# Two token parts of 256 and 288 columns instead of 272 and 272 in a hybrid decoder layer

## The chip, the cores and the metric

The kernel runs on one NeuronCore of a Trainium2 chip. The metric is the device time of one execution in microseconds; the median of three runs before the change is 886.1 us (883.63 to 886.37). TensorE (PE) multiplies matrices, VectorE (DVE) and ScalarE (ACT) do elementwise work and copy results out of PSUM, GpSimd (POOL) does small copies, and SyncE (SP) issues the DMAs.

## The reference

One layer with two gated branches runs side by side on 512 prompt tokens and on 8 x 4 sample tokens (each of 8 requests brings four). Together that is 544 tokens of 1,024 features in float32.

```
shift, scale, gate = split(silu(c) @ w_cond + b_cond, 3)
h = x * (1 + scale) + shift
qa, ka, va, za, qkv_b, zb, a_b, b_b, ga, gb = split(h @ w_in)     # 1024 x 11280
o_a = dilated window attention, 3 groups of 8 heads, mixed by their softmax denominators
o_b = gated delta rule on silu(conv4(qkv_b)), 8 heads of 128, in chunks of 64
ya, yb = o_a * silu(za), rmsnorm(o_b) * silu(zb)
merged = sigmoid(ga) * (ya @ w_branch_a) + sigmoid(gb) * (yb @ w_branch_b)
x = layernorm(ALPHA * x + gate * (merged @ w_out))
```

The new caches and states of both branches are outputs too.

## The kernel before

**Data.** Tokens lie along the free dimension. h is held as two float32r tiles, `hhi` and `hlo` (128 partitions, 8 blocks of features, 544 tokens): the rounded value and the rest. Each weight tile of 128 x 1,024 is split in the same way into `hi` (ScalarE) and `lo` (VectorE). A product in full precision is then three matmuls per block of features: hhi with hi, hlo with hi, hhi with lo.

**Products.** `stream` (line 1043) works through a list of jobs, one for each tile of 128 output columns of `w_in` (85 on h) and one for each tile of the two branch products (8 on `yb`, 8 on `ya`). A job cuts its 544 tokens into two parts of 272 columns, because a `pp` tile has 512 columns. For each part it takes a PSUM bank from `pp` (two banks, lines 36 and 811), runs 8 x 3 matmuls into it (4 x 3 for `ya`), and calls the job's `evac`, which copies or combines the part while the other part runs. The same two parts are used for the first head's three column tiles and the small a/b product at the start (lines 961 to 997).

**What follows a part.** For the convolution (`conv_job`, line 1221 on), part 0 goes to `ext` as 272 columns; part 1 goes as 240 prompt columns and 32 sample columns, which land in another place. For attention (`attention_job`, line 1543 on), queries, keys and values of the prompt go into tiles of 512 tokens, for the two dilated groups in another order of tokens (17 and 15 blocks of 16), and the 32 sample tokens go to `qs`, `ks`, `vs`. Gates and branch products (`za_job`, `zb_job`, `gate_job`, `branch_job`) use `half(t, n)`, the same cut of a 544-wide tile.

**Order.** Every instruction is recorded first. A planner (`schedule`) then simulates all engines with its own cost of each instruction (for a float32r matmul of n columns `0.455e-3 * n + 0.002` us, line 390) and writes out one order per engine. Attention, the delta rule and the gates are generators with ranks; their pieces go between the matmuls of the jobs when their inputs are due. The output product at the end works on 128 tokens at a time, 512 or 256 columns wide, and does not use the two parts.

All instructions are issued by the line 727, which writes the recorded order, so the profile names that line throughout and tiles have to be told apart by name.

Of the kernel before, what the change touches and what calls it, by code (L numbers as in the profile page):

```python
# [13 lines left out]
AF = mybir.ActivationFunctionType  # L14
# [9 lines left out]
NTD = 4  # L24
NS = NB * NTD
NT = SEQ + NS
HF = NT // 2
PROJ = 11280
OFF_Q, OFF_K, OFF_V, OFF_ZA, OFF_B, OFF_ZB, OFF_AB, OFF_GA, OFF_GB = (
    0, 1536, 3072, 4608, 5120, 8192, 9216, 9232, 10256)  # L30
# [749 lines left out]
def body(ctx, tc, io):  # L780
    rec = Recorder()
    pe, ve, se, ge, sp = rec.engines()
# [28 lines left out]
    def pp():  # L811
        return psp.tile([128, 512], F32, name="pp", tag="pp")
# [30 lines left out]
    qs = keep.tile([128, 4, 3, NS], F32, name="qs")  # L843
    ks = keep.tile([128, 4, 3, NS], F32, name="ks")
    vs = keep.tile([128, 4, 3, NS], F32, name="vs")
# [41 lines left out]
    n = CONST[2].shape[1]  # L887
# [4 lines left out]
    abT = op.tile([128, NT], F32, name="abT", tag="o")[0:32]  # L892
    xs = xT[:, :, SEQ:].rearrange("p k (b t) -> p k b t", t=4)
    per_token = lambda t, k, n: t[:, k:k + n, 1:9, None].to_broadcast([128, n, 8, 4])
    cols_of = lambda n: slice(n * HF, (n + 1) * HF)
    with ExitStack() as fctx:
        fr = pool(fctx, "front", 1)
        cT = fr.tile([128, KT, 9], F32, name="cT")
# [59 lines left out]
            return pv[:, :, 0:9], bT[:, 8 * part + at:8 * part + at + m, None].to_broadcast([128, m, 9])  # L958

        x1 = [fr.tile([128, KT, NT], F32R, name=f"x1{u}") for u in "hl"]  # L960
        sums = [[f()[:, :HF] for _ in range(2)] for f in (pp, pd, pg)]
        for b, (c, m) in enumerate(CHUNKS):
            pv, bias = cond_block(1, c, m, b % 2)
            kk = slice(c, c + m)
# [9 lines left out]
            hi, lo = (wsp.tile([128, D], F32R, name=n, tag=n)[:, 0:384 * m].rearrange("p (k c) -> p k c", k=m) for n in ("hi", "lo"))  # L974
            se.activation(hi, W3[:, kk, 0:384], AF.Copy)
            ve.tensor_sub(lo, W3[:, kk, 0:384], hi.bitcast(F32))
            for k in range(c, c + m):
                for t in range(3):
                    w, w_ = (x[:, k - c, 128 * t:128 * t + 128] for x in (hi, lo))
# [7 lines left out]
        hl = fr.tile([128, KT, 32], F32R, name="hl")  # L987
        se.activation(hl[:, :, 0:16], W3[:, :, 384:400], AF.Copy)
        ve.tensor_sub(hl[:, :, 16:32], W3[:, :, 384:400], hl[:, :, 0:16].bitcast(F32))
        ps = [pg(), pg()]  # L990
        for n in range(2):
            for k in range(KT):
                for x in range(2):
                    pe.matmul(ps[n][0:32, :HF], hl[:, k], x1[x][:, k, cols_of(n)],
                              start=(k == 0 and x == 0), stop=(k == KT - 1 and x == 1))
        for n in range(2):
            se.activation(abT[:, cols_of(n)], ps[n][0:32, :HF], AF.Copy)
        for c, m in two_by_two:
            pv, bias = cond_block(0, c, m, c % 4)
            kk = slice(c, c + m)  # L1000
# [2 lines left out]
        ps, pv = pg(), pb_()  # L1003
# [39 lines left out]
    def stream(until):  # L1043

        while done[0] < until:
            i = done[0]
            job = jobs[i]
            for x in range(i, min(i + 5, len(jobs))):
                if x not in raws:
                    raws[x] = wraw.tile([128, D], F32, name="wt", tag="wraw")  # L1050
                    jobs[x].load(raws[x])
                if x <= i + 1 and x not in weights:
                    weights[x] = split(raws[x], jobs[x].nk * 128, ve)
            if job.start:
                yield job.start
            if job.begin:
                job.begin()
            (hi, lo), (xhi, xlo) = weights.pop(i), job.x
            for n in range(2):
                ps = pp()[:, :HF]  # L1060
                cols = slice(n * HF, (n + 1) * HF)
                for k in range(job.nk):
                    a, b = hi[:, k * 128:(k + 1) * 128], lo[:, k * 128:(k + 1) * 128]
                    for w, x in ((a, xhi), (a, xlo), (b, xhi)):
                        pe.matmul(ps, w, x(k)[:, cols], start=(k == 0 and w is a and x is xhi),
                                  stop=(k == job.nk - 1 and w is b))
                    if k < job.nk - 1:
                        yield 0
                job.evac(n, ps)
                if n and job.after:  # L1070
                    job.after()
                if not n:
                    yield 0
            done[0] += 1
            threads.set(job.over, 0.0)
            yield 0
# [4 lines left out]
    def column_job(name, **kw):  # L1081
        return Job(name[0], lambda raw: sp.dma_start(raw, io["w_in"][TILE_AT[name]]), KT, of_h, **kw)

    half = lambda t, n: t[:, n * HF:(n + 1) * HF]


    moves = [(g, b, r, min(r + MOVE, w - 4)) for g, (w, _) in enumerate(GROUPS) for b in range(8) for r in range(0, w - 4, MOVE)]
# [133 lines left out]
    def conv_job(h, s):  # L1221


        hd, tl, t = heads[h], s * 8 + h, {}

        def begin():
            if s == 1:
                hd.cx = dl.tile([128, 81], F32, name="cx")
                hd.stc = dl.tile([128, 3, 8, 3], F32, name="stc")
                sp.dma_start(hd.stc, io["state_conv"][:, h])  # L1230
                hd.KQ = dl.tile([128, 4, 2, 128], F32, name="KQ", bufs=3)
            if s == 2:
                hd.uv = dl.tile([128, 4, 128], F32, name="uv", bufs=1)

        def head_of_ext():
            t["ext"] = ext = dl.tile([128, 571], F32, name="ext")
            ge.memset(ext[:, 0:3], 0.0)
            es = ext[:, 515:571].rearrange("p (b w) -> p b w", w=7)
            ge.tensor_copy(es[:, :, 0:3], hd.stc[:, s])

        def evac(n, ps):
            if not n:
                head_of_ext()
                se.activation(t["ext"][:, 3:275], ps, AF.Copy)
                return
            ext = t["ext"]
            es = ext[:, 515:571].rearrange("p (b w) -> p b w", w=7)
            se.activation(ext[:, 275:515], ps[:, 0:240], AF.Copy)
            se.activation(es[:, :, 3:7], ps[:, 240:272].rearrange("p (b t) -> p b t", t=4), AF.Copy)
            convolve()  # L1250

        def shifted(raw, by):
            head_of_ext()
            ext = t["ext"]
            es = ext[:, 515:571].rearrange("p (b w) -> p b w", w=7)
            ve.tensor_scalar(ext[:, 3:515], raw[:, :SEQ], by[:, 0:1], None, op0=OP.add)
            ve.tensor_add(es[:, :, 3:7], raw[:, SEQ:].rearrange("p (b t) -> p b t", t=4),
                          by[:, 1:9, None].to_broadcast([128, 8, 4]))
            convolve()

        def convolve():
            ext, acc, cx = t["ext"], dl.tile([128, 572], F32, name="acc"), hd.cx
            u = hd.uv if s == 2 else hd.KQ[:, :, 1 - s, :]
            es = ext[:, 515:571].rearrange("p (b w) -> p b w", w=7)
            ge.tensor_copy(cx[:, s:9:3], ext[:, 512:515])
            ge.tensor_copy(cx[:, 9:81].rearrange("p (b t u) -> p u b t", t=3, u=3)[:, s], es[:, :, 4:7])
            se.activation(acc[:, 0:568], ext[:, 0:568], AF.Copy, scale=cw[:, tl, 0:1])
            for i in range(1, 4):
                ve.scalar_tensor_tensor(acc[:, 0:568], ext[:, i:i + 568], cw[:, tl, i:i + 1], acc[:, 0:568],
                                        op0=OP.mult, op1=OP.add)  # L1270
            se.activation(ext[:, 0:568], acc[:, 0:568], AF.Tanh, scale=0.5)
            ve.scalar_tensor_tensor(u, cols128(ext[:, 0:512]), 1.0, cols128(acc[:, 0:512]), op0=OP.add, op1=OP.mult)
            ve.scalar_tensor_tensor(us[:, s, h].rearrange("p (b t) -> p b t", t=4),
                                    win7(ext, 515), 1.0, win7(acc, 515), op0=OP.add, op1=OP.mult)
            if s != 1:
                threads.set(hd.v if s == 2 else hd.kq, 12.0)

        start = ()
        if s == 1 and h > 2:
            start = (heads[h - 3].freed,)  # L1280
        if s == 2 and h:
            start = (heads[h - 1].blocks,)
        job = column_job(("b", h, s), evac=evac, begin=begin, start=start)
        job.shifted = shifted
        return job
# [257 lines left out]
    def attention_job(j, g, s):  # L1543

        def begin():
            pairs[j][s, g] = spare()[:, :SEQ] if s == 2 else ap.tile([128, 512], F32, name="qk"[s], bufs=3)

        def evac(n, ps):
            t, scale = pairs[j][s, g], 1.0 if s else -0.125
            if g == 0:  # L1550
                lo, hi = ((0, 272), (272, 512))[n]
                se.activation(t[:, lo:hi], ps[:, 0:hi - lo], AF.Copy, scale=scale)
            else:
                v = t.rearrange("p (r a n) -> p n a r", r=4, a=4)
                m = (17, 15)[n]
                se.activation(v[:, 17 * n:17 * n + m], ps[:, 0:16 * m].rearrange("p (n a r) -> p n a r", a=4, r=4),
                              AF.Copy, scale=scale)
            if n:
                se.activation((qs, ks, vs)[s][:, j, g if s else at_g(g), :], ps[:, 240:272], AF.Copy, scale=scale)
                if s == 2:  # L1560
                    threads.set(ready[j, g], 2.5)

        return column_job(("a", j, g, s), evac=evac, begin=begin, start=(freed[j - 1] if j else began,))
# [954 lines left out]
```

## Time and profile before

| | |
|---|---|
| three runs | 883.63, 886.1, 886.37 us |
| span of the profiled execution | 886.1 us |
| mean granted TensorE clock | 0.995 |
| DMA, mean rate over the span | 267 GB/s |
| ScalarE activation table loads | 32, 41.1 us |

A group of a profile's page reads: line, engine, operation, output and inputs by the program's names, shape, count, then busy time in us, the mean duration of one in ns, and the engine's idle time just before them with what ended it. "L727 PE MATMUL pp<-hhi,lo" is a matmul into a `pp` bank with `hhi` streaming and `lo` as weights; 128x272 is partitions by columns of the stream. A matmul's duration reaches from its start to its modelled end and overlaps with the next one's. A row of the timeline begins with the start in us from the begin of the span and the duration in us.

### The profile page before, as it was taken

To read this page: it belongs to the slowest core of one execution; us is meant where nothing else is said; L and a number is where in the kernel's file an instruction comes from. 1 tells how busy PE (TensorE), PEld (TensorE's weight loads), DVE (VectorE), ACT (ScalarE), POOL (GpSimd) and SP (SyncE) were. 2 spreads that over 40 slices of the span, in tenths; PEclk is the share of its full clock that TensorE was granted. 3 is DMA by queue.
4 is the path that set the end of the run, shared out by engine and by line. 5 is a ranking of instruction groups with operands and counts; after the bars stand their busy time and mean duration, and the time that the engine had idled before them with its cause. 6 is when DMAs were issued, how large, how long until landed. Compare 5 with 4: busy or idle time off the path is not lost.

```text
span 886.1 us, 20733 instructions
## 1 busy us (share of the span) xinstructions
PE 864.7 (98%) x8176; PEld 818.1 (92%) x8176; DVE 643.4 (73%) x1330; ACT 451.7 (51%) x1073; POOL 68.7 (8%) x167
## 2 busy tenths in 40 slices
PE   8999999999999999999999999999999999999994
PEld 7889999898999899999999988999899999999884
DVE  4675557564458899968999753556899699998547
ACT  3546656765546696347775446732442222324324
POOL 0120110110001110002120000021010000001000
PEclk9999999999999999999999999999999999999998
DMA  9876768666687886889877885479869899987973
GB/s 334 337 212 199 234 219 268 235 206 214 198 256 249 282 278 207 271 265 329 303 227 257 262 291 186 169 219 293 330 223 375 275 402 420 377 285 235 348 248 142
DMA packets 121069, 236.18 MB, mean 267 GB/s; under 512 B 49174, under 2 KB 76640, under 8 KB 118284
## 3 DMA queue, kind: packets, MB, share of 16 engines
q1 hardware_dynamic: 120972, 234.86, 79.0%
q8 instruction: 64, 1.05, 0.5%
q14 instruction: 33, 0.27, 0.1%
HBM read 218.53 MB, written 103.97 MB: 364 GB/s over the span
## 4 chain that ended last, share of the span: by engine, by line
PE 82%; DMA 6%; DVE 5%; ACT 5%; issue 1%; SPq 1%; POOL 0%; DVEq 0%; ACTq 0%
PE pp L727 62%; PE pg L727 9%; PE pd L727 7%; PE pb L727 4%; DMA wc<-in_w_cb 2%; ACT L727 1%; DVE r L727 1%; DMA slab<-in_ks 1%; DMA dO<-orow 1%; DMA S<-in_state_delta 1%; DMA wv<-dw 1%; ACT hi L727 1%; DMA out_kv_s<-in_cache 1%; SPq L727 1%; ACT sq L727 1%
## 5 line engine op out<-in xcount | busy, mean ns | idle before, releaser
L727 PE MATMUL pp<-hhi,hi 128*128 128x272 f32 x1360 | 400.2, 294 | 1.7 <-DVE zt L727 1.0
L727 PE MATMUL pp<-hhi,lo 128*128 128x272 f32 x1360 | 401.3, 295 | 0.0
L727 PE MATMUL pp<-hlo,hi 128*128 128x272 f32 x1360 | 398.1, 293 | 0.0
L727 PEld LDWEIGHTS pp<-hhi,hi 128*128 128x128 f32 x1360 | 257.0, 189 | 4.6 <-issue 1.8
L727 PEld LDWEIGHTS pp<-hhi,lo 128*128 128x128 f32 x1360 | 256.7, 189 | 2.1 <-issue 1.4
L727 PEld LDWEIGHTS pp<-hlo,hi 128*128 128x128 f32 x1360 | 257.1, 189 | 1.5 <-issue 0.4
L727 ACT ACTIVATE hi<-wt 128x1024 fp32r<-128x1024 f32 (+1 forms) x101 | 103.6, 1026 | 171.2 <-PE pp L727 130.1
L727 DVE TENSOR_TENSOR lo<-wt,hi 128x1024 fp32r<-128x1024 f32 (+1 forms) x101 | 119.0, 1178 | 74.9 <-ACT hi L727 74.4
L727 DVE SCALAR_TENSOR_TENSOR acc<-ext,cw,acc 128x568 f32<-128x568 f32 x72 | 58.0, 805 | 1.6 <-ACT acc L727 0.6
L727 DVE TENSOR_TENSOR slab<-slab 128x512 f32<-128x512 f32 (+1 forms) x66 | 43.1, 669 | 6.7 <-DMA slab<-in_ks 4.5
L727 DVE TENSOR_REDUCE slab<-slab 128x8 f32<-128x512 f32 (+2 forms) x66 | 42.7, 660 | 3.3 <-ACT slab L727 3.0
L727 ACT ACT_TABLE_LOAD x32 | 41.1, 1283 | 4.1 <-DMA dO<-orow 1.6
L727 ACT ACTIVATE zt<-pp 128x272 f32<-128x272 f32 x48 | 18.7, 390 | 38.7 <-PE pp L727 37.3
L727 PE MATMUL pp<-ybh,lo 128*128 128x272 f32 x128 | 36.9, 288 | 0.0
L727 PE MATMUL pp<-ybh,hi 128*128 128x272 f32 x128 | 36.9, 288 | 0.0
L727 PE MATMUL pp<-ybl,hi 128*128 128x272 f32 x128 | 36.9, 288 | 0.0
L727 ACT ACTIVATE P<-P,st 128x256 f32<-128x256 f32 (+1 forms) x64 | 31.1, 488 | 11.2 <-DVE st L727 11.1
L727 POOL COPY cx<-ext 128x3 f32<-128x3 f32 (+1 forms) x48 | 21.7, 480 | 151.0 <-ACT ext L727 149.5
L727 DVE CUSTOM_DVE_ANT_0 P<-pg,bias 128x256 f32<-128x256 f32 (+1 forms) x64 | 23.0, 403 | 13.8 <-PE pg L727 13.7
L727 ACT ACTIVATE spare<-pp 128x272 f32<-128x272 f32 (+1 forms) x32 | 16.2, 506 | 16.1 <-PE pp L727 16.1
L727 PEld LDWEIGHTS pp<-ybh,hi 128*128 128x128 f32 x128 | 24.1, 189 | 0.2
L727 PEld LDWEIGHTS pp<-ybh,lo 128*128 128x128 f32 x128 | 24.2, 189 | 0.1
(421 smaller groups left out, 1548.8 us busy)
## 6 DMA issues: line engine op xcount, KB each, us to landing
out_kv_s<-in_cache SPq DMA_DIRECT2D x144, 512.0 KB
wt<-in_w_in SPq DMA_DIRECT2D x85, 512.0 KB
out_kv_s<-in_cache SPq DMA_DIRECT2D x24, 496.0 KB
wc<-in_w_cb SPq DMA_DIRECT2D x16, 512.0 KB
slab<-in_ks SPq DMA_DIRECT2D x32, 256.0 KB
slab<-in_vs SPq DMA_DIRECT2D x32, 256.0 KB
kv<-in_ks SPq DMA_DIRECT2D x16, 512.0 KB
kv<-in_vs SPq DMA_DIRECT2D x16, 512.0 KB
```

The source lines that it names most:

```text
L727: getattr(real[x.engine], x.name)(*map(arg, x.args), **{k: arg(v) for k, v in x.kw.items()})
```

## The change

The cut moves: part 0 holds tokens 0 to 255, part 1 tokens 256 to 543 (256 prompt tokens and the 32 sample tokens). All users of the cut follow. The attention's copies become 256 columns in both parts, and the reordering for the dilated groups has 16 blocks of 16 in each.

```
-HF = NT // 2
+HALVES = (slice(0, 256), slice(256, NT))
+WIDTH = (256, NT - 256)
...
-    cols_of = lambda n: slice(n * HF, (n + 1) * HF)
+    cols_of = lambda n: HALVES[n]
...
-        sums = [[f()[:, :HF] for _ in range(2)] for f in (pp, pd, pg)]
+        sums = [[f()[:, :w] for w in WIDTH] for f in (pp, pd, pg)]
...
-                    pe.matmul(ps[n][0:32, :HF], hl[:, k], x1[x][:, k, cols_of(n)],
+                    pe.matmul(ps[n][0:32, :WIDTH[n]], hl[:, k], x1[x][:, k, cols_of(n)],
...
-                ps = pp()[:, :HF]
-                cols = slice(n * HF, (n + 1) * HF)
+                ps, cols = pp()[:, :WIDTH[n]], HALVES[n]
...
-    half = lambda t, n: t[:, n * HF:(n + 1) * HF]
+    half = lambda t, n: t[:, HALVES[n]]
...
-                se.activation(t["ext"][:, 3:275], ps, AF.Copy)
+                se.activation(t["ext"][:, 3:259], ps, AF.Copy)
...
-            se.activation(ext[:, 275:515], ps[:, 0:240], AF.Copy)
-            se.activation(es[:, :, 3:7], ps[:, 240:272].rearrange("p (b t) -> p b t", t=4), AF.Copy)
+            se.activation(ext[:, 259:515], ps[:, 0:256], AF.Copy)
+            se.activation(es[:, :, 3:7], ps[:, 256:288].rearrange("p (b t) -> p b t", t=4), AF.Copy)
...
-                lo, hi = ((0, 272), (272, 512))[n]
-                se.activation(t[:, lo:hi], ps[:, 0:hi - lo], AF.Copy, scale=scale)
+                se.activation(t[:, 256 * n:256 * n + 256], ps[:, 0:256], AF.Copy, scale=scale)
...
-                m = (17, 15)[n]
-                se.activation(v[:, 17 * n:17 * n + m], ps[:, 0:16 * m].rearrange("p (n a r) -> p n a r", a=4, r=4),
+                se.activation(v[:, 16 * n:16 * n + 16], ps[:, 0:256].rearrange("p (n a r) -> p n a r", a=4, r=4),
...
-                se.activation((qs, ks, vs)[s][:, j, g if s else at_g(g), :], ps[:, 240:272], AF.Copy, scale=scale)
+                se.activation((qs, ks, vs)[s][:, j, g if s else at_g(g), :], ps[:, 256:288], AF.Copy, scale=scale)
```

More of the change, by code (lines that the diff above doesn't have):

```diff
@@ L993, in body @@
                 for x in range(2):
-                    pe.matmul(ps[n][0:32, :HF], hl[:, k], x1[x][:, k, cols_of(n)],
+                    pe.matmul(ps[n][0:32, :WIDTH[n]], hl[:, k], x1[x][:, k, cols_of(n)],
                               start=(k == 0 and x == 0), stop=(k == KT - 1 and x == 1))
         for n in range(2):
-            se.activation(abT[:, cols_of(n)], ps[n][0:32, :HF], AF.Copy)
+            se.activation(abT[:, cols_of(n)], ps[n][0:32, :WIDTH[n]], AF.Copy)
         for c, m in two_by_two:
```

## The prediction

> **What bounds the kernel now.** I read the page first: engines, slices, groups.
>
> ```profile
> span 886.1 us, 20733 instructions
> PE 864.7 (98%) x8176; PEld 818.1 (92%) x8176; DVE 643.4 (73%) x1330; ACT 451.7 (51%) x1073; POOL 68.7 (8%) x167
> PEclk9999999999999999999999999999999999999998
> ...
> L727 PE MATMUL pp<-hhi,hi 128*128 128x272 f32 x1360 | 400.2, 294 | 1.7 <-DVE zt L727 1.0
> L727 PE MATMUL pp<-hhi,lo 128*128 128x272 f32 x1360 | 401.3, 295 | 0.0
> L727 PE MATMUL pp<-hlo,hi 128*128 128x272 f32 x1360 | 398.1, 293 | 0.0
> ...
> L727 PE MATMUL pp<-ybh,lo 128*128 128x272 f32 x128 | 36.9, 288 | 0.0
> ```
>
> TensorE (PE) is occupied 98% of the time at nearly its full granted clock, and in front of the biggest group, 1,360 matmuls, it idled 1.7 us in all. So the time is the time that TensorE takes to work through its list, and a change counts by what it does to that list. The mean of one matmul (294 ns) is not what one costs: three groups of 400 us don't fit beside each other in 886 us, since a matmul begins long before the one ahead of it ends. The cost is the distance from start to start. It comes from the chain of work that ended last, where unbroken runs on the tile pp stand as one piece (start, duration, count):
>
> ```profile
> 359.01 15.73 PE pp L727 x125
> ...
> 375.18 18.12 PE pp L727 x144
> ...
> 486.30 16.73 PE pp L727 x133
> ```
>
> 18.12 us / 144 is 125.8 ns a matmul, and the other two runs also give 125.8. I use that for every 272-wide matmul. How many there are: 3 x 1,360 on hhi and hlo, 3 x 128 on ybh and ybl (one of its three rows is above), and from the groups of TensorE, with shapes kept apart, three groups like the first row here, nine like the second, two like the third (the fourth is used further below):
>
> ```profile
> L727 PE MATMUL pp<-yah,hi 128*128 128x272 f32 x64 | 18.5, 291 | 0.2 <-ACT yah L727 0.2
> L727 PE MATMUL pp<-x1h,hi 128*128 128x272 f32 x16 | 4.4, 308 | 0.3 <-ACT x1h L727 0.3
> L727 PE MATMUL pg<-x1h,hl 128*32 128x272 f32 x16 | 4.1, 286 | 0.0
> L727 PE MATMUL pd<-W,Xc 32*32 32x16 f32 x256 | 3.1, 180 | 1.5 <-issue 1.5
> ```
>
> 4,080 + 384 + 192 + 144 + 32 = 4,832. At 125.8 ns they are 608 us, 69% of the span. The profiled execution's span is 886.1 us and the median of the three runs is 886.1 us, so nothing noticeable lies around the span and I add the sum to 886.1.
>
> **The widths: 2,416 matmuls become narrower by 16 columns, 2,416 wider.** The number of matmuls and weight loads does not change. What matters is whether the distance is a straight line in the width. The last stage (output product) has the same kind of matmul 512 and 256 wide; the timeline of TensorE:
>
> ```profile
> 838.06 0.39 PE L727 MATMUL pp<-wo0l,mhi 128*128 128x512 f32 x1
> ...
> 842.47 0.39 PE L727 MATMUL pp<-wo0h,mlo 128*128 128x512 f32 x1
> 842.69 0.28 PE L727 MATMUL pp<-wo0h,mhi 128*128 128x256 f32 x1
> ...
> 848.27 0.28 PE L727 MATMUL pp<-wo0h,mlo 128*128 128x256 f32 x1
> ```
>
> From the first to the second row are 19 steps: 4.41 us / 19 = 232.1 ns at 512. From the third to the fourth are 47 steps: 5.58 / 47 = 118.7 ns at 256. The line through the two has a slope of 113.4 / 256 = 0.443 ns a column, and at 272 it gives 118.7 + 7.1 = 125.8, exactly the distance measured elsewhere. So 288, which no row shows, should take 125.8 + 7.1 = 132.9 ns. One narrow and one wide matmul together: 118.7 + 132.9 = 251.6 ns; two of 272: 251.6 ns. The term is 0. The starts are printed to 10 ns, 0.2 ns a step over 47 steps, so it is known to about 2,416 x 0.2 = 0.5 us either way.
>
> **The second part's start moves.** The second half of a row of h begins at column 256 instead of 272, 1,024 bytes in instead of 1,088. The timeline shows that the place matters a little. These are the first matmuls of consecutive halves in a stretch that holds nothing else (first, second, first, second half, 24 matmuls each):
>
> ```profile
> 379.28 0.29 PE L727 MATMUL pp<-hhi,hi 128*128 128x272 f32 x1
> ...
> 382.32 0.29 PE L727 MATMUL pp<-hhi,hi 128*128 128x272 f32 x1
> ...
> 385.32 0.29 PE L727 MATMUL pp<-hhi,hi 128*128 128x272 f32 x1
> ...
> 388.36 0.29 PE L727 MATMUL pp<-hhi,hi 128*128 128x272 f32 x1
> ...
> 391.36 0.29 PE L727 MATMUL pp<-hhi,hi 128*128 128x272 f32 x1
> ```
>
> First halves take 3.04 us, second halves 3.00, twice each, with equal widths and equal weights: 0.04 us (known to about 0.01) a product of 48 matmuls, in favour of the start at 1,088 bytes (an odd multiple of 64; the first half's is an even one). If the new start, 1,024, behaves like the first half's, the second half loses that advantage: 85 products on h (4,080 / 48) x 0.04 us = 3.4 us. The start, the PSUM bank and what stands ahead of a half are three possible reasons, which this trace can't tell apart, and only the first moves with the change; nor does anything exclude a start that is better than 1,088. The bounds are 0 and +3.4, and in the other direction what rival A below gives. I take a third of 3.4, +1.1. [...]
>
> **Moving results out of PSUM.** A half that holds keys or queries was copied by ScalarE as 272 and 240 columns and 32 apart, and becomes 256, 256 and 32. From the groups of ScalarE and VectorE:
>
> ```profile
> L727 ACT ACTIVATE q<-pp 128x272 f32<-128x272 f32 x12 | 6.9, 578 | 6.1 <-PE pp L727 4.1 <-DVE ext L727 2.0
> L727 ACT ACTIVATE q<-pp 128x240 f32<-128x240 f32 x12 | 6.3, 522 | 0.6 <-PE pp L727 0.6
> L727 ACT ACTIVATE ext<-pp 128x272 f32<-128x272 f32 x21 | 8.3, 395 | 10.0 <-PE pp L727 9.5 <-DVE KQ L727 0.4
> L727 ACT ACTIVATE ext<-pp 128x240 f32<-128x240 f32 x21 | 7.6, 360 | 0.0
> L727 DVE SCALAR_TENSOR_TENSOR mT<-zt,pp 128x272 f32<-128x272 f32 x16 | 6.9, 431 | 1.4 <-PE pp L727 1.3
> ```
>
> q: 578 + 522 = 1,100 ns becomes twice 550; ext: 755 stays 755. No instruction is added. The second copy ends 28 ns (q) or 18 ns (ext) later behind its product, the gates' and branches' activations and merges 16 columns, about 18 ns. What covers this: there are two pp banks, and the bank is wanted again only after the other half has run, 24 matmuls or 3.0 us later; the 1.7 us of idle time in the first fence is all that TensorE ever waited there. Cost 0. Without that cover it would be at most 100 products x 28 ns = 2.8 us. Only the very last merge stands in the path, 18 ns once.
>
> **The order of the list.** The kernel's planner puts the instructions of all engines in order from its own costs. For these matmuls its cost is also a line in the width, so its total stays, but in its plan each boundary between halves moves 24 x 16 x 0.455 ns = 0.17 us forward. Which small pieces of attention or delta rule go in between will change here and there. Idle time seen in mid-kernel, by waits of TensorE:
>
> ```profile
> PE pd L727 <- issue: 1.5, 1, 1.5
> ...
> PE pg L727 <- ACT P L727: 1.0, 1, 1.0
> PE pp L727 <- DVE zt L727: 1.0, 2, 0.5
> PE pb L727 <- DVE NTs L727: 1.0, 2, 0.5
> PE pb L727 <- DMA S<-in_state_delta: 0.9, 1, 0.9
> ```
>
> Single waits are 0.5 to 1.5 us. New ones will come and old ones go; I take 0, with 2 us either way.
>
> Sum: 0 (widths) + 1.1 (start) + 0 (copies) + 0 (order) = +1.1: **887.2 us**, no change that can be told from none (0.3%, 2.7 us, is about what a measurement of this kernel can tell). This case's own range is 884 to 889.5.
>
> **Rival A, the narrow matmul is faster than the line says.** The last 256-wide matmuls of the kernel run otherwise than the 48 above:
>
> ```profile
> 869.35 0.28 PE L727 MATMUL pp<-wo1h,mhi 128*128 128x256 f32 x1
> ...
> 874.68 0.28 PE L727 MATMUL pp<-wo1h,mlo 128*128 128x256 f32 x1
> ```
>
> 47 steps in 5.33 us: 113.4 ns, 5.3 less, step for step. If all 2,416 narrow ones fell into that stride and the wide ones stayed at 132.9, the gain would be 2,416 x 5.3 ns = 12.8 us: 874.4. If a third of them do, 4.3 us: 882.9. For it: it is the same width and form. Against it: the other 48 did not, although they are as dense; and the first halves on h keep the start that today gives the slower of the two halves. I can't name what separates the two stretches, so it gets 0.2.
>
> **Rival B, slower by one lost window of the clock.** TensorE's granted clock, by stretches (the last three columns are clock, DMA share and GB/s):
>
> ```profile
> 515.00:521.60 6.60, 5.09 (x156) 4.64 (x155) 4.51 (x11) 1.23 (x4) 0.14 (x1) 1.00 0.97 385
> 521.60:525.10 3.50, 3.50 (x36) 3.25 (x37) 2.28 (x6) 0.91 (x1) 0.64 (x2) 0.51 0.69 162
> 525.10:530.00 4.90, 4.90 (x104) 4.55 (x99) 1.50 (x4) 3.11 (x9) 0.00 (x0) 1.00 0.82 239
> ```
>
> Behind the wait of 1.5 us the clock was halved for 3.5 us, which lost 1.7 us; wait and window cost 3.2. If the new order puts one more thin spell of that kind (1.5 us without matmuls decides) into the list, the result is 887.2 + 3.2 = 890.4. For it: the group in front of which the 1.5 us stood has 256 of the smallest matmuls (its row is above, 32x16), which come in several such spells, and their neighbours move. Against it: only one such window fell in the whole run after the start. Chance 0.2. [...]
>
> **Rival C, the change does nothing at all**: the start of the second half doesn't matter, the order stays as good, 886.1. Chance 0.12, which leaves 0.48 for the forecast.
>
> **How the numbers follow.** Faster by over 0.3%: nearly all of A (0.18), the lower edge of the forecast (0.04), a kept window in C (0.03): 0.25. Slower: B (0.19) and the upper edge of the forecast (0.06): 0.25. Within 0.3%: 0.50. The range reaches up to B, 891, and down through the partly filled A, 880; the full A is left out.
>
> **What would show it.** Unbroken runs of the first halves should show 118.7 ns from start to start and those of the second 132.9 (134.6 if the start costs its full 0.04 us a product: 24 x 1.7 ns). 113.4 in the first would be A; 8,176 matmuls must stay, and the pairs of copies must show 256 and 256 with equal means near 550 (q) and 378 ns (ext). A second stretch with a granted clock near 0.5 would be B. The forecast is wrong if the two distances don't add up to 251 to 253 ns, or if they do and the idle time of TensorE moves by more than 2 us.

## The result, and the profile after

The changed kernel takes 892.3 us (median of 4 runs, 889.8 to 895.6), the kernel before beside it 885.1 us: a ratio of 1.0083 [1.0056, 1.0110]. It is slower by 7.2 us, and above the forecast range of 880 to 891. The profiled execution was the shortest of the four (889.8 us, span 888.0), so its trace shows less of the loss than the median has.

The head of the page of after, with the busiest group of matmuls (both widths share the row):

```profile
span 888.0 us, 20738 instructions
PE 865.3 (97%) x8176; PEld 818.8 (92%) x8176; DVE 643.3 (72%) x1329; ACT 455.1 (51%) x1076; POOL 63.6 (7%) x167
...
L728 PE MATMUL pp<-hhi,hi 128*128 128x256 f32 (+1 forms) x1360 | 401.2, 295 | 1.5 <-DVE spare L728 1.0
```

TensorE still is what the time consists of, with the same 8,176 matmuls. The distances from start to start, in the timeline of TensorE in after, one first half, one second half, and the start of the half behind them:

```profile
784.09 0.28 PE L728 MATMUL pp<-hhi,hi 128*128 128x256 f32 x1
...
786.92 0.30 PE L728 MATMUL pp<-hhi,hi 128*128 128x288 f32 x1
...
790.12 0.28 PE L728 MATMUL pp<-yah,hi 128*128 128x256 f32 x1
```

24 narrow ones take 2.83 us (117.9 ns each), 24 wide ones 3.20 (133.3): together 251.2 ns. The mean of all unbroken distances in the products on h is 125.6 ns before, and 118.2 and 133.0 after: 251.2 for a pair both times. So nothing was lost in the distances of these matmuls. The groups of ScalarE show the copies as forecast, near 550 and 378 ns:

```profile
L728 ACT ACTIVATE ext<-pp 128x256 f32<-128x256 f32 x42 | 15.7, 375 | 10.0 <-PE pp L728 9.5 <-DVE KQ L728 0.4
L728 ACT ACTIVATE q<-pp 128x256 f32<-128x256 f32 x24 | 13.1, 546 | 5.9 <-PE pp L728 5.8
```

What is new is in the waits of TensorE in after (us in total, times, longest):

```profile
PE pg L728 <- DVE o L728: 2.8, 1, 2.8
PE pd L728 <- issue: 1.4, 1, 1.4
...
PE pp L728 <- DVE spare L728: 1.0, 1, 1.0
PE pg L728 <- issue: 0.9, 1, 0.9
```

Before, the longest wait after the start was 1.5 us, one that no semaphore ends ("issue"); now there is one of 2.8 behind VectorE, and two of the kind that no semaphore ends. Behind two of these three the clock was halved. In the windows of after, each row is a stretch with the busy time of PE first and the granted clock third from the end:

```profile
421.00:424.20 3.20, 2.04 (x28) 1.91 (x28) 0.52 (x3) 1.47 (x4) 0.00 (x0) 1.00 0.79 207
424.20:427.60 3.40, 3.40 (x21) 2.95 (x18) 3.19 (x13) 2.87 (x11) 0.00 (x0) 0.50 0.96 295
...
792.50:796.28 3.78, 0.95 (x15) 0.48 (x8) 3.10 (x7) 0.00 (x0) 0.00 (x0) 1.00 0.88 301
796.28:799.69 3.41, 3.41 (x17) 3.41 (x17) 1.53 (x7) 0.59 (x4) 0.00 (x0) 0.50 0.69 243
```

Each of these two windows is 3.4 us at clock 0.50 and so loses 1.7 us. Three stalls of 5.1 us and two windows (3.4 us) stand against one stall of 1.5 and one window in the profile of before. That is 5.3 us more, while the two spans differ by only 1.9: smaller waits went, so that TensorE's idle time in all (span less busy time) rose from 21.4 to 22.8 us. In the longer profile of the change shown further below it is 25.8.

### The profile page after: what moved, and what is told of

It reads as the page before. It is cut to its first block, busy times and chain, and to the rows that moved or that the text cites. A ratio compares the mean times of both kernels' runs of the same rounds, so it can differ in the third digit from the quotient of the medians.

```text
span 888.0 us, 20738 instructions
## 1 busy us (share of the span) xinstructions
PE 865.3 (97%) x8176; PEld 818.8 (92%) x8176; DVE 643.3 (72%) x1329; ACT 455.1 (51%) x1076; POOL 63.6 (7%) x167
## 4 chain that ended last, share of the span: by engine, by line
PE 86%; DVE 6%; DMA 4%; ACT 2%; issue 1%; SPq 0%; DVEq 0%; ACTq 0%
PE pp L728 65%; PE pg L728 9%; PE pd L728 8%; PE pb L728 4%; DMA wc<-in_w_cb 1%; DVE r L728 1%; DMA slab<-in_ks 1%; DVE lo L728 1%; DVE od L728 1%; DVE kv L728 1%; DMA wt<-in_w_ga 1%; ACT L728 1%; ACT hi L728 1%; DMA cr<-drows 0%; ACT sq L728 0%
## 5 line engine op out<-in xcount | busy, mean ns | idle before, releaser
L728 PE MATMUL pp<-hhi,hi 128*128 128x256 f32 (+1 forms) x1360 | 401.2, 295 | 1.5 <-DVE spare L728 1.0
L728 PE MATMUL pp<-hlo,hi 128*128 128x256 f32 (+1 forms) x1360 | 399.1, 293 | 0.0
L728 PE MATMUL pp<-hhi,lo 128*128 128x256 f32 (+1 forms) x1360 | 397.1, 292 | 0.0
L728 ACT ACTIVATE zt<-pp 128x256 f32<-128x256 f32 (+1 forms) x48 | 18.8, 391 | 38.9 <-PE pp L728 34.7
L728 PE MATMUL pp<-ybl,hi 128*128 128x288 f32 (+1 forms) x128 | 37.2, 290 | 0.0
L728 PE MATMUL pp<-ybh,hi 128*128 128x288 f32 (+1 forms) x128 | 37.0, 289 | 0.0
L728 PE MATMUL pp<-ybh,lo 128*128 128x288 f32 (+1 forms) x128 | 37.0, 289 | 0.0
L728 DVE CUSTOM_DVE_ANT_0 P<-pg,bias 128x256 f32<-128x256 f32 (+1 forms) x64 | 22.8, 404 | 17.4 <-PE pg L728 17.2
L728 PEld LDWEIGHTS pp<-ybl,hi 128*128 128x128 f32 x128 | 24.1, 188 | 0.1
```

What stands on the lines that cost most here:

```text
L728: getattr(real[x.engine], x.name)(*map(arg, x.args), **{k: arg(v) for k, v in x.kw.items()})
```

## The experiments

Since the planner writes the order from its costs, and these depend on the widths, the change moved two things at once. A helper takes them apart: the program is recorded and planned with one pair of widths (PLAN) and run in that order with another (RUN). Each run is given as its median and its ratio to the kernel before, timed beside it (885.1 to 885.7 us in these series).

**Order or widths (four runs).**

```
+        cut_at(PLAN)
         rec = body(ctx, tc, view)
         rec.schedule()
+        cut_at(RUN)
+        planned, rec = rec, body(ctx, tc, view, rec)
+        rec.follow(planned)
```

> Parts of 256 and 288 as in the change, but every engine's list of instructions in the order that the planner makes for 272 and 272 (the order of before). Theory O, the order: the time lost sits in waits and halved clock that the new order brings, so this kernel runs like before, 884 to 887 us, with one window of half clock in mid-kernel and no wait of more than 1.5 us on TensorE after 700 us. Rival W, the widths: the uneven parts themselves cost (copies of 288 columns, second start at 1,024 bytes), so it stays at 890 to 894 us.

886.6 us, 1.0020 [1.0006, 1.0034].

> Parts of 272 and 272 as before, but in the order that the planner makes for 256 and 288. Theory O: like the change, 889 to 895 us, with the 2.8 us wait of TensorE for the sample attention's result near 793 us. Rival W: like before, 884 to 887 us. If both e1 and e2 come out between, at 887 to 890, order and widths share the loss.

891.9 us, 1.0073 [1.0047, 1.0098].

> The change itself, 256 and 288 in its own order, on the same chip as e1 and e2. Both theories: 890 to 895 us, ratio to before 1.005 to 1.011.

894.5 us, 1.0089 [1.0062, 1.0116].

> Parts of 272 and 272 as before, in the order that the planner makes for parts of 288 and 256: one more draw of an order, with nothing else changed. Theory O: orders differ by several us, so this one lies anywhere between 884 and 896 us and most likely not within 1 us of before. Rival W: 884 to 887 us, since the widths are those of before.

890.8 us, 1.0068 [1.0045, 1.0091].

The order carries about 0.7% (6.5 us) with the old widths, and the order planned for 288 and 256, which nobody chose for its time, costs as much. The widths with the old order carry 0.2% (1.8 us). The waits of TensorE in the first of these, new widths in the old order, lack the 2.8 us:

```profile
PE pp L755 <- DVE zt L755: 1.7, 2, 1.1
PE pb L755 <- DMA wc<-in_w_cb: 1.4, 1, 1.4
PE pd L755 <- issue: 1.1, 1, 1.1
```

The profile of the change run again (895.9 us, span 894.1) is the counterpart of the shorter one above: the same three places, with clock 0.50 behind all of them, behind the first for two windows on end (the page names ScalarE's `slab` for that first wait, 1.9 us in front of the same matmul as in after):

```profile
423.83:430.66 6.83, 6.83 (x45) 5.94 (x43) 3.23 (x13) 3.73 (x12) 0.00 (x0) 0.50 0.63 201
550.12:553.54 3.42, 3.42 (x17) 3.41 (x18) 2.10 (x4) 3.31 (x11) 0.66 (x1) 0.50 0.21 24
802.71:806.12 3.41, 3.41 (x17) 3.41 (x16) 1.21 (x6) 0.59 (x4) 0.00 (x0) 0.50 0.56 215
```

**The wait of 2.8 us near 800 us (four runs).** The timeline of TensorE in after: the last product of the sample attention, and directly behind it in the list a transpose of the value `o` that VectorE makes from it.

```profile
792.08 1.05 PE L728 MATMUL pg<-kv,PTa 128*32 128x256 f32 x16
795.96 0.30 PE L728 MATMUL pg<-cst,o 128*128 128x128 f32 x1 [2.83 <-DVE o L728]
```

I took VectorE's multiplications on `kv` for what makes `o` late.

```
+            if kind == "op" and x.n in leave:
+                continue
```

> The changed kernel with its own order; the last three multiplications on kv that VectorE does in the second half of the sample attention (1.2 us each, in front of the value o that a TensorE transpose waits 2.8 us for at about 796 us) are left out, so that the sample part of branch A isn't the reference's. Theory O, the order (the new order has this piece come due before VectorE has done with it; TensorE waits 2.8 us, and the clock is halved for 3.4 us behind it, 1.7 us lost): wait and window both go, 892.3 - 2.8 - 1.7 = 887.8, between 886.5 and 889.5. Rival D, the drift (the order costs its time in many small places, and the wait only shows a lag that comes out elsewhere): within 1 us of the changed kernel, 891.3 to 893.3.

892.7 us, 1.0072 [1.0049, 1.0096]: no gain, and the wait stays at 2.83 us. That part of theory O fell. The timeline of VectorE in this kernel says why (the last two columns of a row are the idle time and what ended it):

```profile
792.50 1.21 DVE L775 TENSOR_REDUCE od<-kv 128x8 f32<-128x1024 f32 x1
796.23 0.69 DVE L775 TENSOR_TENSOR lo<-wt,hi 128x512 fp32r<-128x512 f32 x1 [2.52 <-ACT hi L775]
796.84 1.21 DVE L775 TENSOR_REDUCE od<-kv 128x8 f32<-128x1024 f32 x1
...
800.85 0.29 DVE L775 TENSOR_TENSOR o<-om 128x128 f32<-128x128 f32 x1
```

VectorE had the time that was saved, and spent it waiting: the split `lo` of the next weights stands in its list ahead of the last two sums over `kv`, and needs `hi` from ScalarE. ScalarE, in its own timeline, waits for TensorE to be done with an earlier tile:

```profile
795.57 0.63 ACT L775 ACTIVATE hi<-wt 128x512 fp32r<-128x512 f32 x1 [2.73 <-PE pp L775]
```

So the chain begins at a matmul of TensorE's own list and runs through `hi`, `lo`, two sums and a few small steps back to TensorE. In the planned order of these lists the wait measured 2.8 us in every profile that put nothing into it. But with all its work done VectorE hardly waits there, as its timeline in after shows:

```profile
790.90 0.69 DVE L728 TENSOR_TENSOR lo<-wt,hi 128x512 fp32r<-128x512 f32 x1 [0.25 <-ACT hi L728]
```

So VectorE's load and this queue hold `o` back for about the same time, and to take away one of them leaves the other.

> The same three multiplications left out of the kernel with the parts of 272 and 272 and its order, as the control (the sample part of branch A isn't the reference's). There TensorE has no wait at that place. Theory O: no change, 884.5 to 886. Rival D: if VectorE's work costs time everywhere, 3 x 1.2 = 3.6 us less, 881.5 to 883.

884.5 us, 0.9987 [0.9970, 1.0005]: no change that can be told from none, as theory O has it for the control.

> The changed kernel with its own order; ten additional 128x128 matmuls on a constant, into unused columns of a PSUM tile, stand in TensorE's list right in front of the transpose that waits at about 796 us (they add work and change no value). Ten of them take 0.7 to 1.2 us, inside the 2.8 us of the wait. Theory O with the window caused by the wait: the transpose starts when it did, the remaining idle stretch is under 2 us, the half-clock window behind it goes: 892.3 - 1.7 = 890.6, between 889.5 and 891. Rival E, the window comes by itself (it is not the wait that sets it off): no change, 891.8 to 893.5, with the clock at 0.5 still there near 796 us.

```
+            if kind == "op" and x is late:
+                extra(x, FILL, 128, 128)
```

892.7 us, 1.0076 [1.0049, 1.0103]. The ten extra matmuls (each is two in the trace) take 2.50 us, not 0.7 to 1.2. They fill the stretch, and the transpose waits only for the rest, 0.31 us:

```profile
796.00 2.50 PE L760 MATMUL pg<-ones 128*128 128x128 f32 x20
798.81 0.33 PE L775 MATMUL pg<-cst,o 128*128 128x128 f32 x1 [0.31 <-DVE o L775]
```

Behind it, from 799.0 to 802.4 us, the clock was 1.00: no window in this profile, as theory O expects. That is little evidence, since of the eight profiles with the whole wait one has no window either. The expected 1.7 us are not to be seen in the median, whose runs lie 8 us apart (886.8 to 895.2): on time this run decides nothing.

```
+            od = [i for i, op in enumerate(dve) if op.name == "tensor_reduce" and named(op, "kv")][-2:]
+            split = [op for op in dve[:od[0]] if op.outs[0].base.kw.get("name") == "lo"][-1]
+            self.pull([dve[i] for i in od], split)
```

> The changed kernel with its own order, the three multiplications on kv left out as before (the sample part of branch A isn't the reference's), and in VectorE's list the last two sums over kv now stand ahead of a split of weights (lo) which waits for ScalarE's rounding of these weights. Theory Q, the queue (leaving out the multiplications alone changed nothing, since VectorE then waited 2.5 us for that split with the sums queued behind it): the wait of TensorE at 796 to 801 us shrinks from 2.8 to about 1.1 us, the time in which VectorE does its last three steps, and the half-clock window behind it goes: 892.7 - 1.7 - 1.7 = 889.3, between 888 and 891. Rival T (TensorE's own last matmul of this piece is what the chain starts from): the wait stays at 2.8 us, 892 to 894.

890.2 us, 1.0039 [1.0017, 1.0061], against 1.0072 without the two lines moved. In its timelines VectorE no longer loses 2.5 us at `lo`, and the wait is about halved:

```profile
796.49 0.69 DVE L795 TENSOR_TENSOR lo<-wt,hi 128x512 fp32r<-128x512 f32 x1 [0.27 <-ACT hi L795]
...
800.20 0.30 PE L795 MATMUL pg<-cst,o 128*128 128x128 f32 x1 [1.49 <-DVE o L795]
```

No window followed in this profile. Theory Q holds for this program, in which VectorE has three multiplications less to do: what kept `o` late there was the queue behind `lo`.

**The two gaps that no semaphore ends (four runs).** The page of after counts the packets of a queue of instructions (packets, MB), and the timeline of TensorE shows the second gap:

```profile
q8 instruction: 64, 1.05, 0.5%
```

```profile
537.37 0.73 PE L728 MATMUL pd<-Tc,NTs 32*32 32x16 f32 x64
538.02 1.09 PE L728 MATMUL pg<-PT,vrow 128*64 128x128 f32 x16
539.05 0.73 PE L728 MATMUL pd<-W,Xc 32*32 32x16 f32 x64
539.70 0.64 PE L728 MATMUL pg<-slab 96*32 96x256 f32 x8
...
541.76 1.14 PE L728 MATMUL pg<-k,q 64*128 64x256 f32 x11
543.81 0.37 PE L728 MATMUL pg<-k,q 64*128 64x128 f32 x1 [0.91 <-issue]
```

64 pieces of 16 KB and 16,352 matmuls and weight loads: if the pieces are TensorE's list, 255.5 of them a piece, so about 256 instructions or 128 matmuls. At 125.6 ns each, 128 matmuls of 272 columns take 16 us; here 144 matmuls went by in 2.33 us (537.37 to 539.70). This row of 212 small matmuls has no wide one in it. In the order for 272 and 272 the 160 on `pd` among them come as 64, 13 wide, 64, 17 wide, 32, and the other 52, of the attention, lie elsewhere. Is the gap a wait for the next piece? The first kernel shifts the list against its pieces.

```
+            if kind == "op" and x is own[0]:
+                extra(x, SHIFT, 32, 8)
```

> The changed kernel with its own order; 32 additional matmuls of 32x8 on a constant stand at the very start of TensorE's list, so that all its later instructions lie 128 places further on (they add work of 1 to 2 us at a place where TensorE waits for the first loads, and change no value). Theory F, fetch (the two gaps of 1.4 and 0.9 us that no semaphore ends, near 424 and 548 us, are waits for the next piece of the instruction list, which is loaded in pieces of fixed length; a burst of the smallest matmuls eats the list faster than it comes): the gaps move to other matmuls or go, the half-clock window near 424 us goes with them, 892.3 - 3 = 889.3, between 888 and 891; the wait at 796 us stays. Rival G, the gaps belong to those matmuls (their own operands): gaps and window stay at the same matmuls, 892 to 894.

899.4 us, 1.0140 [1.0118, 1.0162]. The time went the wrong way: a wait of 3.0 us behind a late DMA near 233 us and a longer second gap came in, which I had not foreseen. But the gap moved to another matmul:

```profile
542.36 0.63 PE L775 MATMUL pg<-slab 96*32 96x256 f32 x4
545.97 0.41 PE L775 MATMUL pg<-slab 96*32 96x256 f32 x2 [2.99 <-issue]
```

It now stands behind 4 of the 8 on `slab` instead of 11 of the 12 on `k,q`, that is 4 + 16 + 32 + 11 = 63 matmuls with their loads earlier, where the shift was 128 instructions. The first gap moved too, to a wide matmul at 418.5 us (1.2 us). So the gaps moved with the shift, to within 2 instructions of the 128 for the second one, and did not stay at their matmuls.

```
+PULL = (3352, 7, 3306), (3374, 6, 3314), (4280, 8, 4206), (4316, 16, 4246)
+        for a, count, to in PULL:
+            self.pull(own[a:a + count], own[to])
```

> The changed kernel with its own order, but for 37 wide matmuls of running products, which TensorE now does inside the two long rows of small ones instead of behind them (13 in the row near 420 us, 24 in the row of 212 near 540 us). All work is done. Theory F, fetch (the gaps of 0.9 to 3.3 us that no semaphore ends come where TensorE works off 128 small matmuls, one piece of its instruction list, faster than the next piece comes): both gaps go, 2.3 to 6.4 us in the profiles so far, and with them the half-clock windows near 424 and 548 us, 1.7 us each in about every second run: 893 - 4 - 1.7 = 887.3, between 886 and 889.5; the wait at 796 us stays. Rival G (the gaps belong to the small matmuls, to their operands or to the DMAs of those stretches): both gaps stay where these matmuls are, 892 to 894.

893.7 us, 1.0082 [1.0051, 1.0112]: no gain, outside what theory F gave. Among the waits of TensorE no "issue" is left, so theory F is right in the place; but what came in their stead near 427 and 549 us is 1.9 us, nearly as long as the 2.3 us of the two gaps in after:

```profile
PE pg L795 <- DVE o L795: 2.8, 1, 2.8
...
PE pg L795 <- DVE st L795: 1.0, 1, 1.0
PE pd L795 <- ACT U L795: 0.9, 1, 0.9
```

I read this so, without a run that shows it: the small products, now later, became late for VectorE and ScalarE, and TensorE waits for these with no wide work left to put in between.

> The kernel with parts of 272 and 272 and its order, but for 25 wide matmuls that are moved into two rows of 64 small ones near 518 us. All work is done. Theory F: the gap of 1.0 to 1.5 us in the second of these rows goes, and the half-clock window behind it where it came: 885.4 - 1.2 - 0.6 = 883.6, between 882.5 and 884.6. Rival G: the gap stays, 885 to 886.

884.8 us, 0.9986 [0.9965, 1.0007].

> Parts of 256 and 288 with the order that was planned for 272 and 272 (the first of these runs, 1.0020 of the kernel before), and the same 25 wide matmuls moved as in the run before this one. Theory F with the widths as measured: as that run, and 1 to 1.8 us more for the widths, 884.6 to 885.6. Rival G: 886 to 887.5.

887.0 us, 1.0009 [0.9990, 1.0028]. In the first of these two the gap near 520 us is gone from the profile, as F has it; in the second one of 0.9 us stands at 527.5. The gain of either is not to be told from none. Between the two stand the widths again, 2.0 us.

**What makes the fetch late (four runs).** SyncE's timeline in after shows what was issued just before the gaps of 422 and 543 us, copies of 512 KB of old cache rows:

```profile
403.89 4.45 SPq L728 DMA_DIRECT2D out_kv_s<-in_cache  x4
...
409.01 1.16 SPq L728 DMA_DIRECT2D out_kv_s<-in_cache  x2
```

```profile
533.15 3.83 SPq L728 DMA_DIRECT2D out_kv_s<-in_cache  x5
```

```
+LATER = tuple((70 + i, 79 + i) for i in range(8)) + tuple((97 + i, 103 + i) for i in range(5))
+        self.later(LATER)
```

> The changed kernel with its own order on TensorE; in SyncE's list 13 of the 168 copies of old cache rows (512 KB each), eight issued between about 404 and 420 us and five between 533 and 543 us, are issued 25 to 50 us later. All work is done. Theory F2 (the piece of TensorE's instruction list comes late since its fetch stands behind these copies in the DMA engines): the two gaps that no semaphore ends, 1.4 to 3.3 us near 424 and 0.9 to 3.1 us near 548, shrink to under 1 us each and their half-clock windows go: 893 - 3 - 1.7 = 888.3, between 887 and 890; the wait near 800 us stays at 2.8. Rival H (128 small matmuls simply go by faster than any fetch comes): both gaps stay, 892 to 894.

889.1 us, 1.0036 [1.0023, 1.0050], inside what F2 gave. TensorE's list is the same to the last matmul, and neither gap is there any more. The longest that are left are the wait near 800 us and one for VectorE's `spare` near 591 us that grew from 1.0 to 2.0 us, with windows of clock 0.50 at both in this profile; its waits begin:

```profile
PE pg L811 <- DVE o L811: 2.8, 1, 2.8
PE pp L811 <- DVE spare L811: 2.0, 1, 2.0
PE pg L811 <- ACT P L811: 1.2, 1, 1.2
```

> As the run before this one, and in VectorE's list the last two sums over kv of the sample attention stand ahead of the split of weights (lo), with all work done. Theories F2 and Q: the wait near 800 us is 1.3 us shorter and its half-clock window goes in most runs: 1 to 2.5 us less than the run before this one, 886.5, between 885.5 and 888.5. If F2 falls and Q holds: 890 to 891.5.

890.4 us, 1.0049 [1.0029, 1.0069]: no better than the run before it. VectorE has no pause in front of `o` any more, but with all its work done it is too late by itself; the wait shrank only to 2.36 us. Neither less load (1.0072) nor a shorter queue alone is worth a measurable gain; with both the ratio was 1.0039. My 886.5 was wrong.

> The kernel with parts of 272 and 272 and its order on TensorE; five of the copies of old cache rows, issued between about 511 and 520 us, are issued 15 us later. Theory F2: the gap of 1.0 to 1.5 us near 520 us goes: 885.6 - 1.2 - 0.5 = 883.9, between 883 and 885. Rival H: 885 to 886.

884.1 us, 0.9992 [0.9977, 1.0008]: the gap of the order before is gone from the profile, the gain too small to tell.

> The changed kernel with its own order, with 64 additional small matmuls on a constant at the very start, each of which is four instructions: everything later lies 256 places further on in TensorE's list. The profile counts 64 fetches of 16 KB for 8,176 matmuls and as many weight loads, so one piece should be 256 instructions. Theory F: the pieces end at the same matmuls as in the changed kernel, so the gaps come back where they were (in front of U,NTs near 424 us and within k,q near 548 us), while with 128 places the second one lay at another matmul; 893 to 896. If the length of a piece isn't 256: both gaps lie elsewhere.

899.1 us, 1.0148 [1.0125, 1.0171]. Shifted by a whole piece, both gaps are back at their old matmuls (timeline of TensorE):

```profile
428.88 1.11 PE L795 MATMUL pd<-U,NTs 64*64 64x64 f32 x16 [2.84 <-issue]
```

```profile
547.03 1.14 PE L795 MATMUL pg<-k,q 64*128 64x256 f32 x11
550.43 0.37 PE L795 MATMUL pg<-k,q 64*128 64x128 f32 x1 [2.25 <-issue]
```

Again 11 of 12, as without a shift, which fits a piece of 256 instructions. The time is above what I expected: at the same matmuls this profile is 5.3 us later (547.03 against 541.76), more than I had assumed for the extra ones, and both gaps were longer in it.

The packets of queue q8 in the traces bear theory F out. Between 20 and 870 us the profiles of all runs have 20 waits of over 0.7 us that no semaphore ends. Counted over TensorE's loads and matmuls in order of start, all 20 stand 79 to 117 places into a piece of 256, and 19 of them end 1.2 to 1.6 us after a piece has landed (the other 0.6 us). The gap of before stands 83 places into a piece and ended 1.28 us after a landing, those of after 105 and 81 places and 1.37 and 1.20 us. In after one piece landed at 542.6 us, and TensorE went on at 543.8. For F2: the transfer of that piece began when TensorE had started 10,554 loads and matmuls, and 10,403 in the run with the 13 copies later, so it came earlier in the list.

**All three places at once (two runs).**

> The changed kernel with its own order on TensorE and all three causes treated at once: the 13 copies issued later, the two sums ahead of the split of weights, and the three multiplications on kv left out (the sample part of branch A isn't the reference's). If the three places are what the order costs: the 4 us of the copies and the 2.5 us of the queue add up, 893 - 4 - 2.5 = 886.5, between 885.5 and 888, level with the run after this one to 1.5 us. If something else of the order costs time too: 888.5 to 890.

885.7 us, 1.0007 [0.9991, 1.0024].

> Parts of 256 and 288 with the order planned for 272 and 272, and five copies of old cache rows issued 15 us later, as in the run that did this for the kernel before (0.9992). Widths alone cost 1.1 to 1.8 us: 884.1 + 1.4 = 885.5, between 884.5 and 886.8.

885.5 us, 1.0009 [0.9994, 1.0025]. The two orders are level. The waits of TensorE in the first of these two, where the three new ones had stood:

```profile
PE pg L811 <- DVE o L811: 1.5, 1, 1.5
PE pp L811 <- DVE spare L811: 1.4, 1, 1.4
```

So the late fetches and the wait for `o`, for which VectorE's load and the queue behind `lo` had to be treated together, are with their windows what the new order costs, to about 1.5 us, the width of these intervals; the three multiplications left out in the first are worth about 1 us of it by their control (0.9987, within its interval). No version beats the kernel before by more than its interval; the nearest are that kernel with the copies later (0.9992) or with wide matmuls moved (0.9986).

## Why the prediction was wrong

- **The base, 886.1.** Nothing noticeable was to lie around the span. The timed execution of after has 1.8 us there (889.8 against 888.0), so by this estimate the profile of before is one of 887.9 us, longer than any of the four timed beside it. No term hangs on it, but the two profiles differ by less than the two kernels do.
- **Widths, 0.** Right for the distances: 118.2 and 133.0 ns add up to 251.2, as two of 125.6 do, and rival A's 113.4 did not come.
- **Start of the second part, +1.1.** The size is near what the widths cost (1.4 to 2.0 us in four pairs of runs with the same order, all of one sign, though not each beyond its interval). That is luck, since the place was wrong: the sum of the distances did not grow, 251.2 ns before and after. Where the 1.4 to 2.0 us lie, I did not find.
- **Copies, 0.** Right: 546 and 375 ns, and among the long waits none for a copy.
- **Order, "I take 0, with 2 us either way".** This step failed. It measured 6.5 us. I had argued from the planner's total, which stays, and from single waits of 0.5 to 1.5 us seen before, as if new ones came and went alike. Three waits came that reach 2.8 to 3.3 us where they are longest. Two of them the total leaves out, since the planner has no cost for the pieces of the instruction list: behind 144 small matmuls in 2.33 us TensorE stood in after until 1.20 us after a piece had landed, and with 13 copies issued later neither gap came. In the third, TensorE comes to the transpose of `o` 2.8 us before VectorE has made it. Behind two of the three in after came a window of 1.7 us besides. What changed in the lists is whether wide matmuls come between the small ones, and how many copies are issued in a bunch.
- **Rival B** had the spells of small matmuls and the windows behind them and was under-sized: not one more thin spell of 3.2 us but three places with 5 to 9 us of stalls (5.1 in the profile of after, 9.2 in that of the run without the multiplications) and two to four windows in the two profiles of the change. Its point from which it decides, 1.5 us without matmuls, stood on the one stall and window of before and is not one: over all profiles, between 20 and 870 us, a window began at 3 of the 9 stalls of 1.4 to 1.5 us and at 18 of the 25 of 1.9 to 3.3 us (at most 2.3 us behind the stall), and the longest, 3.26 us, had none. The stall of 2.8 us near 800 us had one in 7 of 8 profiles.
- **The spread.** That one program has a window in one run and not in the next, on which the chance of 0.03 for a kept window in C rests, is not shown by the one profile of before. The runs of the change show it: two windows in one profile (888.0 us, mean granted clock 0.993) and four in the other (894.1, 0.989). A range of 11 us was wide enough in itself; it lay too low.

## What to carry to other kernels

Where a planner's costs or sizes are touched, the new order is a new draw, and it should be priced like an edit: run the old order with the new sizes, and the other way round, before looking at sizes at all. On an engine that is 98% busy, read each idle time over 1 us from the list around it: what stands ahead of the late instruction on its own engine (taking work away there brought no gain here, 1.0072, as the queue waited for something else), how many small instructions come in a row, and what was handed to the DMA queues just before.

## What the runs showed of the hardware

- In before and after, queue q8 moved 64 pieces of 16 KB of instructions for 16,352 matmuls and weight loads of TensorE, 255.5 a piece; shifted by 128 instructions the gaps that no semaphore ends lay at other matmuls, shifted by 256 at the old ones. In after one such gap followed 144 small matmuls in 2.3 us. In all profiles 20 of them were over 0.7 us (0.8 to 3.3), 79 to 117 places into a piece, and 19 ended 1.2 to 1.6 us after a piece had landed. With 13 copies of 512 KB issued later, the same list had none of the two of after.
- The half-clock windows in mid-kernel came as 3.41 us or twice that (6.83), each at clock 0.50, and began at 18 of 25 stalls of 1.9 to 3.3 us and 3 of 9 of 1.4 to 1.5. One stall of 2.8 us, filled with matmuls on a constant, had no window behind it; one of eight that were not filled had none either.
- In the products on h, 272 columns took 125.6 ns from start to start in before, 256 took 118.2 and 288 took 133.0 in after: a line with 0.46 ns a column.
